# Hybrid decoder step: the samples' reads of the SSD and matrix states with each state as the weights

## The chip, the cores and the metric

The kernel runs on one NeuronCore of one Trainium2 chip, and what is measured is the device time of the whole program in microseconds (us). Before the change it is 1962.44 us, the median of 3 runs (1961.87 to 1963.68).

The engines are named as the profile names them: PE is TensorE's matrix product and PEld its weight load (a second row of the same engine, which runs beside PE), DVE is VectorE, ACT is ScalarE, POOL is GpSimd, and SP is SyncE, which issues the transfers. A matrix product `mm(out, lhsT, rhs)` loads `lhsT` as the weights and streams the columns of `rhs` past them into a PSUM bank.

## The reference, cut to what matters

The program computes one layer of a hybrid decoder: a norm, one wide input projection, two groups of heads side by side (32 SSD heads and 8 mLSTM heads), an output projection, and a gated feed-forward part with a short convolution. It does so for one prompt of 272 tokens (16 learned ones and 256) and for 8 samples of 8 tokens each. The samples carry states of earlier tokens, and this case is about how a sample's tokens read their state:

```python
# SSD, per chunk: Cc are the tokens' read vectors, S the carried state
y = y + jnp.einsum('btgn,bgepn,btge->btgep', Cc, S, jnp.exp(cum))
# mLSTM, per chunk: qc the queries, Cp the carried matrix state, wi the inter-chunk factor
num = jnp.einsum('btsh,bshv->bthv', W, vc) + wi[..., None] * jnp.einsum('bthd,bhdv->bthv', qc, Cp)
```

For a sample b, a head's 8 read vectors (128 long) are multiplied by that sample's own state. The SSD state of two heads is 128 x 128 (128 state entries, 2 x 64 channels), and the matrix state of an mLSTM head is 128 x 256. Every sample has another state, so no two samples share a weight matrix.

## The kernel before

Activations lie transposed: 128 channels on the partitions, 336 tokens as columns. Columns 0 to 255 are the prompt, columns 256 to 319 (`NP` to `ND`) the 64 sample tokens, 8 for each sample, and the rest the learned tokens. All large products are done by `gemm`: a weight block of 8 tiles of 128 x 128 is loaded, ACT and DVE split it into a high and a low part (tiles `hi` and `lo`), and PE runs three products for each tile. These write the banks named `g`. The pool `wp` holds three blocks, and `Feed.next` splits two blocks ahead.

The work of the heads is written as Python generators. `gemm` calls `tick` after every fourth tile, and each tick lets each live generator issue one step, so its small matrix products stand in PE's queue between two groups of `gemm` products. PE and SP keep the order in which the program is written (`manual_schedule`); the instructions of DVE, ACT and POOL are ordered by a scheduler. A small product therefore costs PE its own time, and where it waits, everything behind it on PE waits too.

An mLSTM head (`head`, 8 of them, about 40 to 437 us of the span) makes its read in three places. `spread` on POOL copies the 64 scaled query columns into `qp`, a tile with 32 columns for each sample of which 8 are filled. `read` issues 8 products with `qp[:, b, :]` as weights and the 256 columns of sample b's state as moving columns; four samples fill the four 32-partition strips of one bank `st`, and the second four add to them. ACT copies the bank to `ys`. One step later `turned` transposes the two halves of `ys` on PE, and ACT picks the 64 columns that matter into `yst`. Much later in the head the sums of prompt and samples are made in the two banks `pn` (tag `nm`), and DVE adds `yst` to the sample columns of each.

An SSD unit (`unit`, two heads, 16 of them, about 437 to 800 us) does the same with the state tile `S0` (named S in the profile) and the tile `cp`, which `group` fills once for 8 units: 8 products into a bank `st`, a copy to `ys`, and two steps later one transpose into the bank `pe`, which DVE multiplies into the sample columns of the factor `E`. PE then puts the two products of the prompt's states `S1` and `S2` into the other columns of `pe`, and DVE multiplies those into `E` in a second instruction.

Of the kernel before, what the change touches and what calls it, by code (L numbers as in the profile page):

```python
# [9 lines left out]
F32 = mybir.dt.float32  # L10
F32R = mybir.dt.float32r
AF = mybir.ActivationFunctionType
ALU = mybir.AluOpType
ADD, SUB, MUL, MAX, MIN = ALU.add, ALU.subtract, ALU.mult, ALU.max, ALU.min

P = 128
# [5 lines left out]
NB, TS = 8, 8  # L22
T = TP + NB * TS
NP = 256
NQ = 322
ND = 320
# [23 lines left out]
def hymba_kernel(ctx, tc, cst, xT, w0, w1, wo, wu, wd, shist, s0, c0n, fhist,  # L50
                 yT, conv_o, ssd_o, c_o, m_o, ffn_o):
    nc = tc.nc
    uid = [0]

    def tl(pool, shape, dt=F32, tag=None, **kw):
        uid[0] += 1
        return pool.tile(shape, dt, tag=tag, name=f"{tag}_{uid[0]}", **kw)
# [10 lines left out]
    def mm(out, lhsT, rhs, start=True, stop=True):  # L68
        nc.tensor.matmul(out, lhsT, rhs, start=start, stop=stop)  # L69

    def tt(out, a, b, op):
        nc.vector.tensor_tensor(out, a, b, op=op)  # L72
# [7 lines left out]
    def act(out, a, f, **kw):  # L80
        nc.scalar.activation(out, a, f, **kw)  # L81

    def bank(pool, n, tag="g"):
        return tl(pool, [P, 512], tag=tag)[:, :n]
# [6 lines left out]
    def C(name, i=0, n=None):  # L91
        o, w = _CST[name]
        return cs[:, o + i:o + (w if n is None else i + n)]
# [86 lines left out]
    def start(gen, half=1):  # L180
        gens.append((gen, half))
        next(gen)
# [78 lines left out]
    a = []  # L261
# [26 lines left out]
    with ExitStack() as pa:  # L288
        ca = pa.enter_context(tc.tile_pool(name="ca", reuse_waits="tile", bufs=1))
        pt = pa.enter_context(tc.tile_pool(name="pt", reuse_waits="tile", bufs=1, space=bass.MemoryType.PSUM))  # L290
        pm = pa.enter_context(tc.tile_pool(name="pm", reuse_waits="tile", bufs=2, space=bass.MemoryType.PSUM))
# [17 lines left out]
        sv = lambda t: t[:, NP:ND].rearrange("p (b t) -> p b t", b=NB)  # L309
# [157 lines left out]
            for i in range(2):  # L467
                mm(ps, onesr, x[i], start=i == 0, stop=i == 1)

        def spread(dst, src):  # L470

            nc.gpsimd.tensor_copy(dst[:, 0:4, 0:TS], sv(src)[:, 0:4])
            nc.gpsimd.tensor_copy(dst[:, 4:8, TS:2 * TS], sv(src)[:, 4:8])

        def read(cp, states, n):

            pc = bank(pm, n, "st")
            for b in range(NB):
                o = 32 * (b % 4)
                mm(pc[o:o + 32], cp[:, b, :], states[:, b, :n], start=b < 4, stop=b >= 4)  # L480
            return pc

        def turned(ys, pst=None):

            n = ys.shape[1] // P
            pst = tl(pt, [P, 4, P], tag="tr") if pst is None else pst
            for i in range(n):
                nc.tensor.transpose(pst[:, i, :], ys[:, i * P:(i + 1) * P], C("ident"))
            v = pst[:, :n, :].rearrange("p i (b u t) -> p i u b t", u=4, t=TS)
            return [v[:, i, :2] for i in range(n)]  # L490

        def stacked(d, x, second):

# [9 lines left out]
        def mstack(dst, src, n, second):  # L503

            stacked([dst[32 * i:32 * i + 16, :n] for i in range(3)], src[64:80, 2, :n], second)

        def sb(t):
            return t.rearrange("p (s b t) -> p s b t", s=2, t=TS)

        def masked(dst, src):  # L510
            n = src.shape[2]
# [14 lines left out]

        steps = {-1: 99}

        def heads(ml, qps, h, kf, qf, v0, v1):
            while not gates_done or steps.get(h - 1, 0) < 9:  # L530
                yield
            for n, _ in enumerate(head(ml, qps, h, kf, qf, v0, v1)):
                steps[h] = n
                yield

        def head(ml, qps, h, kf, qf, v0, v1):
            C0 = tl(ml, [P, NB, 257], tag="C0", bufs=2)
            nc.sync.dma_start(C0, c0n[h])
            rowB = tl(ml, [P, 3, T], tag="rowB")
            nc.sync.dma_start(rowB, scr_m[h].unsqueeze(0).to_broadcast([P, 3, T]))  # L540
            qp = qps[h % 2]
            dm = dec[:, 32 + h, :]
            vtok = tl(ml, [P, 3, 258], tag="vtok")
            ksc = tl(ml, [P, 3, P], tag="ksc")
# [10 lines left out]
            act(D[:80, 256:NQ], D[:80, 256:NQ], AF.Exp)  # L555
            qwi = B()
            gt(qwi[:, :ND], qf[:, :ND], rowB[:, 1, :ND], MUL)
            spread(qp, qwi)
            yield

            pq = tl(pt, [P, 4, P], tag="tr").rearrange("p a b -> p (a b)")
# [14 lines left out]
            transpose3(v0, lambda ap, r, c: act(vtok[r, c, 0:128], ap, AF.Copy))  # L576
            yield
            transpose3(v1, lambda ap, r, c: act(vtok[r, c, 128:256], ap, AF.Copy))

            ys = tl(ml, [P, 256], tag="ys")  # L580
            act(ys, read(qp, C0, 256), AF.Copy)
            yield
            yst = tl(ml, [P, 2, 64], tag="yst")
            for i, v in enumerate(turned(ys)):
                act(sb(yst[:, i, :]), v, AF.Copy)

            C1 = tl(ml, [P, 257], tag="C1")
            C2 = tl(ml, [P, 257], tag="C2")
# [23 lines left out]
            for i in range(2):  # L612
                pn = bank(pm, NQ, "nm")
                vs = slice(128 * i, 128 * i + 128)
                for c, (o, n, w) in enumerate(WC):
                    mm(pn[:, o:o + w], vtok[:n, c, vs], W[:n, o:o + w], start=c == 0, stop=False)
                mm(pn[:, 0:128], C1[:, vs], qwi[:, 0:128], start=False, stop=False)
                mm(pn[:, 128:256], C2[:, vs], qwi[:, 128:256], start=False)
                tt(pn[:, NP:ND], pn[:, NP:ND], yst[:, i, :], ADD)
                nums.append(pn)  # L620
                q = B()[:, :NQ]
                act(q, pn, AF.Square)
                sq.append(q)
                yield
# [41 lines left out]
                yml[2 * h + i] = split(yh[i])  # L666

        with tc.tile_pool(name="ml", reuse_waits="tile", bufs=1) as ml:
            qps = [tl(ml, [P, NB, 32], tag=f"qp{i}") for i in range(2)]
            kmt = tl(ml, [80, P], F32R, tag="kmt")  # L670
            vmt = tl(ml, [80, 258], F32R, tag="vmt")
            for t_ in qps + [kmt.bitcast(F32), vmt.bitcast(F32)]:
                nc.gpsimd.memset(t_, 0.0)

            def kqv(h):
                fe = []
                for i, ti in enumerate(KQV(h)):
                    n = NQ if i == 1 else T
                    ps = inproj(ti, n, *((pm, "nm") if h + i == 0 else ()))
                    f = B()[:, :n]  # L680
                    tt(f, ps, R[:, :n], MUL)
                    fe.append(f)
                start(heads(ml, qps, h, *fe), h % 2)

            def oevac(h, i, ps):
                while not ready:
                    yield
                o_ = B()[:, :NQ]
                tt(o_, ps, Rh[:, :NQ], MUL)
                act(o_, o_, AF.Tanh)  # L690
                og[h, i] = o_
                yield

            def ogate(h):
                for i, ti in enumerate(OG(h)):
                    start(oevac(h, i, inproj(ti, NQ)))

            for i in range(2):
                start(oevac(0, i, first[1 + i]))
            for x in stream:  # L700
                (ogate if x[0] == "o" else kqv)(int(x[1]))
            early = {ti: inproj(ti) for ti in (1,)}
            while gens:
                tick()
# [4 lines left out]
        with tc.tile_pool(name="sd", reuse_waits="tile", bufs=1) as sd:  # L709
# [49 lines left out]
            def group(bc, out):  # L759
                for _ in range(3):  # L760
                    yield
                bf, cf = bc
                pq = tl(pt, [P, 4, P], tag="tr").rearrange("p a b -> p (a b)")
                for c, (o, n, w) in enumerate(WC):
                    mm(pq[:n, o:o + w], bf[:, o:o + n], cf[:, o:o + w])
                cb = tl(sd, [P, T], tag="cb")
                tt(cb[:, :256].rearrange("p (c t) -> p c t", c=2),
                   pq[:, :256].rearrange("p (c t) -> p c t", c=2),
                   C("mask").unsqueeze(1).to_broadcast([P, 2, P]), MUL)
                tt(cb[:80, 256:NQ], pq[:80, 256:NQ], C("mask2")[:80, :66], MUL)  # L770
                cp = tl(sd, [P, NB, 32], tag="cp")
                nc.gpsimd.memset(cp, 0.0)
                spread(cp, cf)
                out += [cb, cf, cp]
                yield
                bt = tl(sd, [P, 3, P], tag="bt")
                transpose3(bf, lambda ap, r, c: copy(bt[r, c, :], ap))
                act(bmt[64:80], bt[64:80, 2, :], AF.Copy)
                out.append(bt)

            def unit(j, gc, pad, ps, zz):
# [6 lines left out]
                nc.sync.dma_start(S0, s0[j])  # L788
                yield

                cb, cf, cp = gc[:3]
                Dm = tl(sd, [P, 2, T], tag="Dm")
                hs = slice(2 * j, 2 * j + 2)
                for hh in range(2):
# [6 lines left out]
                tt(Dm[:80, :, 256:NQ], Dm[:80, :, 256:NQ],  # L801
                   cb[:80, None, 256:NQ].to_broadcast([80, 2, 66]), MUL)
                yield
                bt = gc[3]

                xp = tl(sd, [P, 3, P], tag="xp")
                xw = tl(sd, [P, 3, P], tag="xw")
# [21 lines left out]
                act(E[0:64], cmb[0:64, 0, :ND], AF.Exp)  # L829
                act(E[64:128], cmb[64:128, 1, :ND], AF.Exp)  # L830
                yield
                ys = tl(sd, [P, P], tag="ys")
                act(ys, read(cp, S0, P), AF.Copy)
                pi = bank(pm, NQ, "nm")
                for c, (o, n, w) in enumerate(WC):
                    for hh in range(2):
# [21 lines left out]
                   .to_broadcast([P, NB, 2, 64]), MUL)  # L858
                yield
                yield  # L860
                es = sb(E[:, NP:ND])
                pe = bank(pm, 512, "nm")
                tt(es, es, turned(ys, pe[:, 256:384].rearrange("p (a b) -> p a b", a=1))[0], MUL)
                mm(pe[:, 0:128], S1, cf[:, 0:128])
                mm(pe[:, 128:256], S2, cf[:, 128:256])
                tt(E[:, :256], E[:, :256], pe[:, :256], MUL)
                pps = [tl(pm, [P, 512], tag="st").rearrange("p (a b) -> p a b", a=4) for _ in range(2)]
                for i, pp in enumerate(pps):
                    rows = slice(32 * i, 32 * i + 32)
# [274 lines left out]
```

## Time and profile before

| | |
|---|---|
| median of 3 runs | 1962.44 us |
| the profiled execution | 1962.04 us, span 1960.3 us |
| PE busy / PEld busy | 1929.2 us (98%) / 1891.2 us (96%) |
| DVE / ACT / POOL busy | 1240.5 (63%) / 856.3 (44%) / 381.5 us (19%) |
| granted TensorE clock, mean | 0.997 |
| HBM | 162 GB/s over the span |

The span is what the profile sees between the first and the last instruction; 1.7 us of the profiled execution lie around it. A matrix product in plain fp32 is one instruction of the program and shows as two records in the trace, each with its own weight load. The records of PE overlap, since they include the time in the pipe, so the time that a product takes from its successors is read from the distance between starts and not from the length of a record. "x16" at a row's end counts records, and `nm<-cf,S` reads: written bank, then the moving operand, then the weights.

### The profile page before, as it was taken

Reading aid. Unit: us, or ns where it says so; the run is one execution under the profiler, and the core shown is the slowest. Engines: PE = TensorE matmul, PEld = TensorE weight load, DVE = VectorE, ACT = ScalarE, POOL = GpSimd, SP = SyncE. Lnnn points to the kernel's source line nnn. Section 1 sums busy time; section 2 is a strip of 40 time slices with the busy share of each in tenths; the row PEclk is TensorE's granted clock in tenths of the full one; section 3 lists DMA queues with packets and bytes.
Section 4 is the critical chain, followed back from the end, with each engine's and each line's share of the span. In section 5 each row is a group of like instructions: output and inputs, shape, how many; then the busy total and the mean of one; then the engine's idle time right before and its main releaser. Section 6 shows DMA issues by size and latency. Waiting matters only on the chain.

```text
span 1960.3 us, 33606 instructions
## 1 busy us (share of the span) xinstructions
PE 1929.2 (98%) x13302; PEld 1891.2 (96%) x13302; DVE 1240.5 (63%) x2064; ACT 856.3 (44%) x1301; POOL 381.5 (19%) x721
## 2 busy tenths in 40 slices
PE   9999999999999999999999999999999999999997
PEld 8999999999989998999999999999999999999997
DVE  7877676777888788655547666655555556333344
ACT  6355555555444455433334444443334435333332
POOL 1211111212434343211112111111111110111111
PEclk9999999999999999999999999999999999999998
DMA  7545555546554655455554444444444444555553
GB/s 228 178 150 191 175 174 179 193 156 204 185 182 162 199 178 180 150 161 157 163 165 145 154 146 149 153 153 150 148 153 151 152 147 150 148 150 151 152 148 113
DMA packets 94221, 319.68 MB, mean 163 GB/s; under 512 B 10680, under 2 KB 19440, under 8 KB 92016
## 3 DMA queue, kind: packets, MB, share of 16 engines
q1 hardware_dynamic: 93744, 317.26, 50.7%
q8 instruction: 104, 1.70, 0.4%
q10 hardware_dynamic: 320, 0.28, 0.1%
q14 instruction: 53, 0.43, 0.1%
HBM read 294.80 MB, written 22.70 MB: 162 GB/s over the span
## 4 chain that ended last, share of the span: by engine, by line
PE 94%; DVE 3%; DMA 1%; issue 1%; ACT 1%; SPq 0%; DVEq 0%; ACTq 0%
PE g L69 87%; PE st L69 3%; PE nm L69 2%; DMA rowB<-scr_m 1%; PE tr L458 1%; DVE lo L72 1%; DVE blk L78 0%; DVE yb L72 0%; ACT hi L81 0%; DVE blk L72 0%; DMA raw<-in_w 0%; DVE co L78 0%; DVE pad L72 0%; DVE blk L552 0%; PE tr L69 0%
## 5 line engine op out<-in xcount | busy, mean ns | idle before, releaser
L69 PE MATMUL g<-blk,hi 128*128 128x322 f32 (+2 forms) x6240 | 1429.5, 313 | 0.0
L69 PEld LDWEIGHTS g<-blk,hi 128*128 128x128 f32 x6240 | 1054.1, 189 | 5.5 <-issue 4.8
L72 DVE TENSOR_TENSOR lo<-raw,hi 128x1024 fp32r<-128x1024 f32 (+3 forms) x509 | 652.6, 1282 | 464.6 <-ACT hi L81 459.5
L69 PE MATMUL g<-blk,lo 128*128 128x322 f32 (+2 forms) x2992 | 930.8, 311 | 0.0
L81 ACT ACTIVATE hi<-raw 128x1024 fp32r<-128x1024 f32 (+2 forms) x507 | 527.6, 1041 | 760.7 <-PE g L69 521.4
L69 PEld LDWEIGHTS g<-blk,lo 128*128 128x128 f32 x2992 | 563.8, 188 | 0.0
L69 PE MATMUL g<-ah,hi 128*128 128x322 f32 (+1 forms) x832 | 259.6, 312 | 0.0
L69 PE MATMUL g<-ah,lo 128*128 128x322 f32 (+1 forms) x832 | 259.5, 312 | 0.0
L69 PE MATMUL g<-al,hi 128*128 128x322 f32 (+1 forms) x832 | 258.8, 311 | 0.0
L69 PEld LDWEIGHTS g<-ah,hi 128*128 128x128 f32 x832 | 158.2, 190 | 0.1
L69 PEld LDWEIGHTS g<-al,hi 128*128 128x128 f32 x832 | 157.3, 189 | 0.1
L69 PEld LDWEIGHTS g<-ah,lo 128*128 128x128 f32 x832 | 157.1, 189 | 0.0
L72 DVE TENSOR_TENSOR fpad<-g,R 128x256 f32<-128x256 f32 (+2 forms) x264 | 54.6, 263 | 95.2 <-PE g L69 95.1
L235 POOL TENSOR_TENSOR blk<-h 128x322 f32<-128x322 f32 (+1 forms) x28 | 31.0, 1107 | 400.1 <-DVE h L72 231.8
L78 DVE SCALAR_TENSOR_TENSOR fcv<-fpad,fc,fcv 128x336 f32<-128x336 f32 x176 | 99.4, 567 | 3.9 <-ACT fcv L81 0.8
L976 POOL COPY fo<-fpad 128x2 f32<-128x2 f32 x88 | 17.5, 199 | 338.7 <-DVE fpad L72 338.6
L81 ACT ACTIVATE blk<-blk 128x322 fp32r<-128x322 f32 (+6 forms) x118 | 50.4, 450 | 51.7 <-DVE blk L78 20.9
L75 POOL TENSOR_TENSOR blk<-fsg,fcv 128x256 f32<-128x256 f32 x88 | 46.6, 553 | 112.2 <-PE g L69 60.9
L81 ACT ACTIVATE fcv<-fpad,fc 128x336 f32<-128x336 f32 x88 | 57.2, 652 | 0.1
L81 ACT ACTIVATE fsg<-fcv 128x336 f32<-128x336 f32 x44 | 21.3, 484 | 73.1 <-DVE fcv L78 73.1
L236 POOL TENSOR_TENSOR acc<-acc,blk 128x322 f32<-128x322 f32 (+2 forms) x46 | 51.8, 1126 | 2.5
L72 DVE TENSOR_TENSOR blk<-blk,blk 128x322 fp32r<-128x322 f32 (+3 forms) x76 | 38.9, 522 | 18.4 <-ACT blk L81 18.0
(212 smaller groups left out, 1340.0 us busy)
## 6 DMA issues: line engine op xcount, KB each, us to landing
raw<-in_wu SPq DMA_DIRECT2D x176, 512.0 KB, 3.7
raw<-in_w SPq DMA_DIRECT2D x164, 512.0 KB, 4.1
raw<-in_wd SPq DMA_DIRECT2D x80, 512.0 KB, 3.6
raw<-in_wo SPq DMA_DIRECT2D x64, 512.0 KB, 4.1
out_c_o<-co SPq DMA_DIRECT2D x8, 1156.5 KB, 7.4
out_ssd_o<-so SPq DMA_DIRECT2D x16, 576.0 KB, 3.7
C<-in_c0n SPq DMA_DIRECT2D x8, 1028.0 KB, 6.6
S<-in_s SPq DMA_DIRECT2D x16, 512.0 KB, 4.9
```

What stands on the lines that cost most here:

```text
L69: nc.tensor.matmul(out, lhsT, rhs, start=start, stop=stop)
L72: nc.vector.tensor_tensor(out, a, b, op=op)
L75: nc.gpsimd.tensor_tensor(out, a, b, op=op)
L78: nc.vector.scalar_tensor_tensor(out, a, s, b, op0=op0, op1=op1)
L81: nc.scalar.activation(out, a, f, **kw)
L235: eng.tensor_tensor(q, x, x, op=MUL)
L236: eng.tensor_tensor(self.acc[eng], self.acc[eng], q, op=ADD)
L458: nc.tensor.transpose(pst[:n, c, :], src[:, o:o + n], C("ident"))
L976: nc.gpsimd.tensor_copy(fo[:, li, 0:2], pad[:, 256:258])
```

## The change

The tiles `qp`, `cp`, `ys` and `yst` go, with the functions that fill and turn them. A new function `reads` takes each sample's state as the weights (128 x 128) and that sample's 8 tokens as the moving columns, and writes them where the sums stand: 8 products for each half of an mLSTM head, added to the bank `pn`, and 8 products for each SSD unit, into the sample columns of `pe`. In the unit they stand at the step where the old read stood; `pe` is therefore taken at that step, and the product with `E` becomes one DVE instruction over all 320 columns.

```diff
-        def spread(dst, src):
-            nc.gpsimd.tensor_copy(dst[:, 0:4, 0:TS], sv(src)[:, 0:4])
-            nc.gpsimd.tensor_copy(dst[:, 4:8, TS:2 * TS], sv(src)[:, 4:8])
-
-        def read(cp, states, n):
-            pc = bank(pm, n, "st")
+        def reads(ps, states, x, first=True):
             for b in range(NB):
-                o = 32 * (b % 4)
-                mm(pc[o:o + 32], cp[:, b, :], states[:, b, :n], start=b < 4, stop=b >= 4)
-            return pc
-
-        def turned(ys, pst=None):
-            n = ys.shape[1] // P
-            pst = tl(pt, [P, 4, P], tag="tr") if pst is None else pst
-            for i in range(n):
-                nc.tensor.transpose(pst[:, i, :], ys[:, i * P:(i + 1) * P], C("ident"))
-            v = pst[:, :n, :].rearrange("p i (b u t) -> p i u b t", u=4, t=TS)
-            return [v[:, i, :2] for i in range(n)]
+                t = slice(NP + b * TS, NP + b * TS + TS)
+                mm(ps[:, t], states[:, b, :], x[:, t], start=first and b == 0, stop=b == NB - 1)
...
             transpose3(v1, lambda ap, r, c: act(vtok[r, c, 128:256], ap, AF.Copy))
-            ys = tl(ml, [P, 256], tag="ys")
-            act(ys, read(qp, C0, 256), AF.Copy)
-            yield
-            yst = tl(ml, [P, 2, 64], tag="yst")
-            for i, v in enumerate(turned(ys)):
-                act(sb(yst[:, i, :]), v, AF.Copy)
+            yield
...
                 mm(pn[:, 0:128], C1[:, vs], qwi[:, 0:128], start=False, stop=False)
-                mm(pn[:, 128:256], C2[:, vs], qwi[:, 128:256], start=False)
-                tt(pn[:, NP:ND], pn[:, NP:ND], yst[:, i, :], ADD)
+                mm(pn[:, 128:256], C2[:, vs], qwi[:, 128:256], start=False, stop=False)
+                reads(pn, C0[:, :, vs], qwi, False)
...
-                ys = tl(sd, [P, P], tag="ys")
-                act(ys, read(cp, S0, P), AF.Copy)
+                pe = bank(pm, ND, "nm")
+                reads(pe, S0, cf)
                 pi = bank(pm, NQ, "nm")
...
-                es = sb(E[:, NP:ND])
-                pe = bank(pm, 512, "nm")
-                tt(es, es, turned(ys, pe[:, 256:384].rearrange("p (a b) -> p a b", a=1))[0], MUL)
                 mm(pe[:, 0:128], S1, cf[:, 0:128])
                 mm(pe[:, 128:256], S2, cf[:, 128:256])
-                tt(E[:, :256], E[:, :256], pe[:, :256], MUL)
+                tt(E, E, pe, MUL)
```

On PE, in a head's first half of the sums (`nm`), between two groups of `gemm`, these rows stood before:

```order
L69 MATMUL g_1805<-blk_160,lo_1678 128x336
L69 MATMUL st_1836<-vtok_1509,ksc_1510 128x257
L69 MATMUL nm_1839<-blk_1615,vtok_1509 128x128 x2
L69 MATMUL nm_1839<-blk_1615,vtok_1509 128x66
L69 MATMUL nm_1839<-blk_1564,C_341_1774 128x128
L69 MATMUL nm_1839<-blk_1564,C_342_1775 128x128
L69 MATMUL g_1805<-blk_173,hi_1727 128x336
```

At the same place of PE's order the changed kernel has:

```order
L69 MATMUL g_1777<-blk_160,lo_1667 128x336
L69 MATMUL st_1808<-vtok_1500,ksc_1501 128x257
L69 MATMUL nm_1811<-blk_1604,vtok_1500 128x128 x2
L69 MATMUL nm_1811<-blk_1604,vtok_1500 128x66
L69 MATMUL nm_1811<-blk_1555,C_331_1746 128x128
L69 MATMUL nm_1811<-blk_1555,C_332_1747 128x128
L69 MATMUL nm_1811<-blk_1555,C_286_1496 128x8 x8
L69 MATMUL g_1777<-blk_173,hi_1705 128x336
```

One row of 8 products with 8 columns each has come in, behind the prompt's two (C_286 is the samples' state tile, C_331 and C_332 are the prompt's); the second half of the head has the same row. The two places of a head where `read` and `turned` stood have lost their rows.

On PE, in an SSD unit, at the step of the read, these rows stood before (S_980 is the samples' state tile, `Dm` and `xp` belong to the unit's own sums):

```order
L69 MATMUL g_5439<-blk_232,lo_5388 128x322
L69 MATMUL st_5509<-S_980_5335,cp_5283 32x128 x8
L69 MATMUL nm_5519<-Dm_5375,xp_5417 64x128 x4
L69 MATMUL nm_5519<-Dm_5375,xp_5417 64x66 x2
L69 MATMUL st_5526<-xw_5418,bmt_5062 128x128
```

At this place the changed kernel has:

```order
L69 MATMUL g_5391<-blk_232,lo_5340 128x322
L69 MATMUL nm_5460<-cf_5109,S_945_5287 128x8 x8
L69 MATMUL nm_5469<-Dm_5327,xp_5369 64x128 x4
L69 MATMUL nm_5469<-Dm_5327,xp_5369 64x66 x2
L69 MATMUL st_5476<-xw_5370,bmt_5018 128x128
```

The 8 products stay where they were in the order, with weights and moving operand exchanged: 128 weight columns in place of 32, 8 moving columns in place of 128.

On PE, two steps later in the same unit, with the engines that each row waits for, before:

```order
L69 MATMUL g_5555<-blk_232,lo_5479 128x336
L488 MATMUL nm_5628<-cs_71,ys_5508 128x128 [waits Activation_49]
L69 MATMUL nm_5628<-cf_5153,S_1011_5530 128x128 [waits DVE_49,Activation_49]
L69 MATMUL nm_5628<-cf_5153,S_1012_5531 128x128
L69 MATMUL st_5634<-xm_5427,bt_5322 128x512 [waits PE_49,Pool_49]
L69 MATMUL st_5635<-xm_5427,bt_5322 128x512 [waits PE_49]
```

And in the changed kernel:

```order
L69 MATMUL g_5505<-blk_232,lo_5431 128x336
L69 MATMUL nm_5460<-cf_5109,S_975_5480 128x128 [waits Activation_49]
L69 MATMUL nm_5460<-cf_5109,S_976_5481 128x128 [waits DVE_49]
L69 MATMUL st_5581<-xm_5379,bt_5274 128x512 [waits Pool_49]
L69 MATMUL st_5582<-xm_5379,bt_5274 128x512 [waits DVE_49,PE_49]
```

The transpose is gone, and the product with the first prompt state no longer waits for DVE. The product with the second one (S_976, which DVE writes) and the second product into a bank `st` carry waits for DVE now.

## Rows read from the trace of the kernel before

**Rows 1.** The page: busy time, share of the span and instruction count of each engine, and the chain of work that ended last by engine.

```profile
PE 1929.2 (98%) x13302; PEld 1891.2 (96%) x13302; DVE 1240.5 (63%) x2064; ACT 856.3 (44%) x1301; POOL 381.5 (19%) x721
PE 94%; DVE 3%; DMA 1%; issue 1%; ACT 1%; SPq 0%; DVEq 0%; ACTq 0%
```

**Rows 2.** Busy time by stretch, the mLSTM heads and the SSD units: the stretch in us, its length, then busy us (and instructions) of PE, PEld, DVE, ACT and POOL, the granted TensorE clock, DMA share, GB/s.

```profile
40.00:437.00 397.00, 394.60 (x2752) 385.56 (x2751) 290.39 (x514) 206.36 (x372) 69.15 (x109) 1.00 0.53 174
437.00:800.00 363.00, 352.53 (x2609) 327.04 (x2608) 300.22 (x595) 179.55 (x344) 138.58 (x176) 1.00 0.55 181
```

**Rows 3.** Groups of PE instructions by line and shape: weights' rows*columns, moving operand's shape, record count, then busy us, mean ns of one record, idle time before them.

```profile
L69 PE MATMUL st<-S,cp 128*32 128x128 f32 x256 | 10.3, 279 | 0.0
L69 PE MATMUL st<-C,qp 128*32 128x256 f32 x128 | 8.6, 385 | 0.0
L488 PE MATMUL nm<-cs,ys 128*128 128x128 f32 x16 | 4.3, 270 | 0.0
L488 PE MATMUL tr<-cs,ys 128*128 128x128 f32 x16 | 3.1, 272 | 0.0
```

**Rows 4.** PE in order of time in head 1, at the step that transposes the first half of the values: start us, length us, engine, line, operation, operands, shape, records. `g` rows are `gemm`.

```profile
94.12 0.31 PE L69 MATMUL g<-blk,lo 128*128 128x322 f32 x1
94.27 0.49 PE L458 MATMUL tr<-cs,blk 128*128 128x128 f32 x3
94.52 0.55 PE L69 MATMUL g<-blk,hi 128*128 128x322 f32 x2
94.90 0.31 PE L69 MATMUL g<-blk,lo 128*128 128x322 f32 x1
```

**Rows 5.** The same view at the next step of the same head, which transposes the second half of the values and then makes the old read.

```profile
98.00 0.31 PE L69 MATMUL g<-blk,lo 128*128 128x322 f32 x1
...
98.57 1.07 PE L69 MATMUL st<-C,qp 128*32 128x256 f32 x16
99.58 0.56 PE L69 MATMUL g<-blk,hi 128*128 128x322 f32 x2
99.98 0.31 PE L69 MATMUL g<-blk,lo 128*128 128x322 f32 x1
```

**Rows 6.** PEld, the weight loads, in order of time in the first half of the sums of head 1: the last two loads of the products with the values `vtok`, then four with the prompt's states, then `gemm`.

```profile
108.35 0.30 PEld L69 LDWEIGHTS nm<-blk,vtok 80*128 80x128 f32 x2
...
108.57 0.53 PEld L69 LDWEIGHTS nm<-blk,C 128*128 128x128 f32 x4
109.02 0.30 PEld L69 LDWEIGHTS g<-blk,hi 128*128 128x128 f32 x2
```

**Rows 7.** PE beside it: the two records of the product with 66 moving columns, and the first of the next product.

```profile
108.46 0.34 PE L69 MATMUL nm<-blk,vtok 80*128 80x66 f32 x2
108.63 0.33 PE L69 MATMUL nm<-blk,C 128*128 128x128 f32 x1
```

**Rows 8.** PE in order of time at the read of the first SSD unit.

```profile
477.70 0.30 PE L69 MATMUL g<-blk,lo 128*128 128x322 f32 x1
477.94 0.64 PE L69 MATMUL st<-S,cp 128*32 128x128 f32 x16
478.51 0.78 PE L69 MATMUL nm<-Dm,xp 128*64 128x128 f32 x12
```

**Rows 9.** PE in order of time two steps later in the same unit, at the transpose of the read; in brackets idle time before, and what ended it.

```profile
487.19 0.32 PE L69 MATMUL g<-blk,lo 128*128 128x336 f32 x1
487.35 0.27 PE L488 MATMUL nm<-cs,ys 128*128 128x128 f32 x1
488.31 0.68 PE L69 MATMUL nm<-cf,S 128*128 128x128 f32 x4 [0.69 <-DVE pad L72]
488.93 1.13 PE L69 MATMUL st<-xm,bt 32*128 32x512 f32 x4
```

**Rows 10.** What PE waited for in the whole span: us in total, times, longest us.

```profile
PE nm L69 <- DVE pad L72: 9.0, 14, 0.7
PE tr L458 <- DVE blk L72: 2.0, 3, 1.1
...
PE nm L69 <- DVE E L72: 1.5, 2, 1.1
```

**Rows 11.** Groups of weight loads by shape: rows*columns of the weights, record count, busy us, mean ns of one record. L488 is a transpose, where the data are the weights.

```profile
L69 PEld LDWEIGHTS nm<-cf,S 128*128 128x128 f32 x64 | 8.3, 190 | 14.5 <-issue 13.1 <-ACT hi L81 1.3
...
L488 PEld LDWEIGHTS nm<-cs,ys 128*128 128x128 f32 x16 | 2.3, 141 | 0.0
```

**Rows 12.** Busy time by stretch, columns as in rows 2: a wait of PE among the heads, and two stretches at the program's end. The granted clock is the third number from the right.

```profile
178.00:181.00 3.00, 1.92 (x14) 1.67 (x13) 3.00 (x8) 1.50 (x5) 1.07 (x2) 1.00 0.22 79
1945.00:1950.00 5.00, 1.34 (x6) 0.61 (x5) 4.73 (x8) 0.79 (x2) 2.27 (x2) 1.00 0.13 49
1950.00:1953.00 3.00, 0.00 (x0) 0.00 (x0) 2.97 (x4) 0.00 (x0) 1.51 (x2) 0.55 0.84 314
```

**Rows 13.** PE in order of time at the program's start: the 12 products that only warm the engine.

```profile
1.17 3.69 PE L69 MATMUL g<-R 128*128 128x336 f32 x12 [1.17 <-POOL R L98]
```

**Rows 14.** The chain that ended last, in order of time: the `gemm` products behind the block of rows 9 (start us, us, what).

```profile
490.53 7.09 PE g L69 x48
```

**Rows 15.** DVE in order of time beside rows 9, and, earlier, at the writing of the second prompt state `S2` (named S).

```profile
482.10 0.46 DVE L78 SCALAR_TENSOR_TENSOR S<-S,dec,st 128x64 f32<-128x64 f32 x2
...
487.96 0.21 DVE L72 TENSOR_TENSOR E<-E,nm 128x64 f32<-128x64 f32 x1
```

## The prediction before the run

> **What bounds the kernel now.** Read the page's first lines first: PE is busy for 98% of the span, and the chain of work that ended last runs over PE for 94% [rows 1]. The view by stretches says the same of the two stages that the change touches: PE is busy for 394.6 of 397 us among the heads and for 352.5 of 363 among the SSD units, while DVE, ACT and POOL have room [rows 2]. So a microsecond that is put into PE's queue or taken out of it appears in the time, and work taken from ACT and POOL (the copies to ys and yst, spread) and the additions on DVE are worth nothing by themselves. Of PE's 10.5 idle us in the SSD stage, nearly all are one wait in each unit [rows 10], at one place [rows 9]. For all else the question is only how long PE works on the old read and on the new one. For that I read the distance between gemm products on both sides of a block, in the view in order of time. A gemm product takes 0.148 us of PE: 48 of them fill 7.09 us [rows 14].
>
> **Heads: what goes.** Two steps of head 1 differ only in the old read. The step without it spans 0.78 us, from the gemm product at 94.12 to the one at 94.90 [rows 4]; the step with it spans 1.98 us, from 98.00 to 99.98 [rows 5]. The read takes 1.20 us, 9.6 in 8 heads. It is cheap because four samples stand in four strips: 16 records of 256 columns need about one us. The three transposes of rows 4 take 0.78 - 3 x 0.148 = 0.34 us, 0.11 each. The 16 transposes of ys [rows 3], two in a head, take 2 x 0.11 x 8 = 1.8 us. Together 11.4 us go.
>
> **Heads: what comes.** A product in fp32 has two records: the old read's 8 products in each of 8 heads are 128 records [rows 3]. The new 16 products of a head are therefore 32 weight loads of 128 columns and 32 runs of 8 columns, and 256 of each in all heads. No row of before has 8 moving columns, so I bound the pair. Beside a product with 66 columns the two weight loads start 0.22 us apart from what follows, 0.11 each (108.35 to 108.57), and the four loads of products with 128 columns take 0.45 us, again 0.11 each (108.57 to 109.02) [rows 6, 7]. Halving the columns did not shorten the pair: the load sets the pace there, and 8 columns hide behind it just as 66 do. I take 0.111 us, the mean of these six (0.67 / 6 = 0.112, rounded down for the two digits of the rows). The lower bound is the weight load of a transpose, whose record is 141 ns against 190 ns for an ordinary one [rows 11]: 0.049 us less, 0.06 for a pair. The upper bound is a whole load's record with nothing beside it, 0.19 us. I choose 0.111 because rows 6 show the same shape, type and neighbour (the new reads stand right behind these four loads), and the upper one would need loads that never overlap, which rows 6 exclude for their case. 256 x 0.111 = 28.4 us. Heads: +28.4 - 11.4 = +17.0 us.
>
> The Trainium skill says otherwise of such pairs: its page "TensorE: Matmul & The Clock Gate", section "Back-to-back issue gap", gives about 81 ns for a sustained stream of weight load and product with 128 columns. The rows here have 111 ns for it; the sum would be about +3.6 us by 81 ns, and the measurement decides.
>
> **SSD units: the read.** Before, from the last gemm product to the unit's own products: 477.70 to 478.51, 0.81 us [rows 8]. Of the 0.24 us in front of the first strip, 0.148 belong to gemm and 0.09 to the change to strips, which the unit's products (two strips) still pay. After: 0.15 for gemm, 15 steps of 0.111 = 1.67 from the first read to the last, 0.01 for its 8 columns, 0.09 for strips: 1.92 us, 1.11 more. 16 units: +17.7 us.
>
> **SSD units: the transpose and its wait.** Before, from 487.19 to the products with xm at 488.93: 1.74 us, of which 0.69 are PE's wait [rows 9]. The row names DVE's pad, but what PE needs is the product with E that reads the transposed block out of pe: it runs on DVE from 487.96 for 0.21 us [rows 15], and PE goes on 0.1 us behind it. After the change nothing of this step reads pe before PE has written it. Left are 0.16 for gemm's product, 4 x 0.111 for the two products, 0.09 for the strips of xm: 0.69 us. So 0.36 us go beside the wait, 5.7 in 16 units, and the waits themselves, 9.0 + 1.5 us [rows 10]: 16.2 in all. What is late next? The second prompt state is written by DVE at 482.10 [rows 15], 5 us early, and the new wait of a product with xm is for an st bank whose readers on DVE belong to the same early group. DVE's order also changes: the products with E and the two sums now stand ahead of a split into lo; 48 gemm products, 7.09 us [rows 14], lie between this place and the first use of that split in PE's order. I price both at nothing; if that cover were gone, the wait would come back (below). SSD: +17.7 - 16.2 = +1.5 us.
>
> **The sum.** +17.0 + 1.5 = +18.5 us on the profiled execution's 1962.04 us (span 1960.3 and 1.7 around it) gives 1980.5. The median of the runs is 0.4 above that execution, so 1981 us, 0.9% slower. The ends: 0.108 us a pair gives +17.0, and the 2.0 us that PE waits at the heads' transposes [rows 10] may vanish or double, since DVE's order and the arrival of transfers shift: 1977. With the 8 columns never hidden (0.111 + 0.007 = 0.118) it is +22.0, with 2 us of waits 1986.5.
>
> **Rivals.**
> *Loads get quick when almost no columns stream beside them (faster than before).* At 0.06 us a pair, as the transposes' loads suggest [rows 11], the heads have +15.6 - 11.4 = +4.2; a unit's read is 0.25 + 15 x 0.061 - 0.81 = +0.36, 5.7 in 16, against 16.2: -10.5. Sum -6.3, 1956 us. It decides from the point where a pair falls under 0.074 us: the sum is 496 pairs (256 and 16 x 15) less 36.6 us (11.4, 16.2 and 16 x 0.56), and is zero there. For it: transposes do it. Against it: rows 6 show no shortening at 66 columns, and the new weights are ordinary ones. 6%. Halfway, at 0.086 us, the sum is +6.1, 1968.5 us, and up to 0.082 us it would be within the bound of no change. 6%, of which 4 lie there. By the 81 ns of the Trainium skill's "TensorE: Matmul & The Clock Gate" ("Back-to-back issue gap") this case would end at 1966 us.
> *The wait is replaced.* If PE must wait as long for DVE at the second state, the st bank or the later split as it did for E, the 10.5 us are not won: 1991.5 us. For it: two new waits in the order, and DVE is busy for 300 of the 363 us [rows 2]. Against it: the times above. 5%.
> *The clock falls.* In a stretch of 16 pairs PE streams almost nothing for 1.8 us. At the program's start the lower of the two levels, 1.2 GHz, shows: 12 products with 336 columns in 3.69 us, 0.31 each, about twice what gemm pays [rows 13]. If after each of the 32 blocks 12 gemm products ran at that level, 32 x 12 x 0.15 = 58 us are added: 2039. Against it: among the heads PE stood idle for 1.1 us of 178 to 181 us at a granted clock of 1.00, and at the end it is still 1.00 over 1945 to 1950, with PE busy for 1.34 of 5 us, before it falls to 0.55 [rows 10, 12]. 4%.
> *Loads and columns do not overlap at all*, 0.19 us a pair: heads +48.6 - 11.4, units 16 x 2.29 - 16.2, sum +57.6, 2020 us. 3%.
>
> **How the numbers follow.** The forecast keeps 76%; its own range is 1977 to 1986.5. The range that should hold the time 8 times in 10 takes in the wait that comes back and some error in the entry to each block: 1974 to 1992. No change means within 0.2%, 3.9 us, about what a measurement of this kernel can tell. Faster by more: 6%, the quick loads. Within: 4%, the part of the halfway case. Slower: 90%.
>
> **What the profile after would show.** Right: in PEld's rows the loads of nm<-blk,C with 128 columns and 8 moving ones follow each other at 0.11 us, and a unit's read block (gemm to Dm) lasts 1.9 us where it was 0.8; PE's wait at the products with cf is gone from the waits; the stretch of the heads is 17 us longer, that of the units 1 or 2. Wrong: loads at 0.06 or 0.08 us; a new wait of PE for DVE at cf or xm, which would put the units' stretch at +10 or more; a granted clock under 1.00 among the heads; or gemm products that start later than their predecessors ask, which would mean that a block of weights came late.

## The result and the profile after

The changed kernel takes 1983.12 us, the median of 4 runs (1982.64 to 1984.08), against 1962.54 us for the kernel before on the same chip (4 runs, 1961.87 to 1963.68). The ratio is 1.0105 with a 95% interval of 1.0087 to 1.0122: slower by 20.6 us, or 17 to 24 by the interval. The profiled execution took 1982.78 us with a span of 1980.7. Its page, busy time by engine and the chain that ended last, answers to [rows 1]:

```profile
PE 1960.7 (99%) x13398; PEld 1938.6 (98%) x13398; DVE 1225.7 (62%) x2032; ACT 851.1 (43%) x1261; POOL 398.0 (20%) x697
PE 94%; DVE 3%; DMA 2%; ACT 1%; issue 1%; SPq 0%; DVEq 0%; ACTq 0%
```

DVE and ACT have less to do than before (14.8 and 5.2 us less), and the program is longer all the same: PE is the engine that counts, and its weight loads are busy for 47 us more. The weight loads of PE in the first half of the sums of head 1 answer to [rows 6]; the 20 loads are the prompt's four and the 16 new ones:

```profile
106.75 2.31 PEld L69 LDWEIGHTS nm<-blk,C 128*128 128x128 f32 x20
108.98 0.30 PEld L69 LDWEIGHTS g<-blk,hi 128*128 128x128 f32 x2
```

From the first of the 20 to the load of gemm lie 2.23 us, 0.1115 for each. This is the price that the four loads of [rows 6] had (0.1125), although 16 of the 20 now have only 8 columns behind them. PE at the read of the first SSD unit answers to [rows 8]:

```profile
494.69 0.31 PE L69 MATMUL g<-blk,lo 128*128 128x322 f32 x1
494.83 1.85 PE L69 MATMUL nm<-cf,S 128*128 128x8 f32 x16
496.61 0.78 PE L69 MATMUL nm<-Dm,xp 128*64 128x128 f32 x12
```

1.92 us lie between the gemm product and the unit's own products, where it was 0.81. Two steps later the transpose of [rows 9] and the wait behind it are gone:

```profile
505.32 0.31 PE L69 MATMUL g<-blk,lo 128*128 128x336 f32 x1
505.47 0.60 PE L69 MATMUL nm<-cf,S 128*128 128x128 f32 x4
506.00 1.13 PE L69 MATMUL st<-xm,bt 32*128 32x512 f32 x4
```

That is 0.68 us up to the products with xm, where it was 1.74. What PE waits for now, in the whole span (us, times, longest), answers to [rows 10]:

```profile
PE tr L458 <- DVE blk L72: 1.8, 2, 1.0
PE nm L69 <- DVE lo L72: 1.6, 2, 1.0
...
PE st L69 <- DVE vmt L72: 0.4, 1, 0.4
...
PE st L69 <- ACT vs L81: 0.3, 1, 0.3
```

The two lines for the SSD units (9.0 and 1.5 us) have no successor. The two lines for `st` are new and small: they stand at the product with vmt of two heads. The stretch that holds both sums of head 1, and one with a unit's read (columns as in [rows 12], the granted clock third from the right), show that the clock did not move:

```profile
100.00:115.00 15.00, 15.00 (x114) 14.89 (x112) 7.40 (x12) 6.51 (x12) 0.14 (x2) 1.00 0.33 108
495.00:500.00 5.00, 5.00 (x47) 4.91 (x47) 2.56 (x10) 3.56 (x10) 1.93 (x1) 1.00 0.61 206
```

How far the kernel has fallen behind is read from the chain that ended last. Three of its runs of gemm products stand at the same places of both kernels: ahead of the heads' reads, behind the heads, and behind the last unit (start us, us, what). In the kernel before:

```profile
39.74 32.76 PE g L69 x216
...
436.75 21.99 PE g L69 x144
...
798.91 1145.82 PE g L69 x7734
```

In the changed kernel, where the last run is broken once:

```profile
39.41 32.69 PE g L69 x216
...
453.71 21.94 PE g L69 x144
...
817.75 207.07 PE g L69 x1391
...
1026.76 4.09 DMA fpad<-in_xT
...
1030.94 0.51 DVE h L72
...
1032.74 932.71 PE g L69 x6294
```

The changed kernel starts 0.33 us early, is 16.96 us late behind the heads and 18.84 us late behind the last unit: the heads took 17.3 us more and the units 1.9. The break is the turn from the output projection to the up projection. There PE had to wait for the last residual tile of x, whose transfer was issued 0.7 us later against the gemm products than before (1026.76 us here, 1007.18 there, less the 18.84); against the same gemm products in the trace of before it costs 0.8 us. The rest of the 20.4 us between the two spans, 0.8, is spread thinly over the gemm products behind it, and is no more than what the runs of one kernel differ by.

### The profile page after: what moved, and what is told of

It reads as the page before. It is cut to its first block, busy times and chain, and to the rows that moved or that the text cites. A ratio compares the mean times of both kernels' runs of the same rounds, so it can differ in the third digit from the quotient of the medians.

```text
span 1980.7 us, 33680 instructions
## 1 busy us (share of the span) xinstructions
PE 1960.7 (99%) x13398; PEld 1938.6 (98%) x13398; DVE 1225.7 (62%) x2032; ACT 851.1 (43%) x1261; POOL 398.0 (20%) x697
## 4 chain that ended last, share of the span: by engine, by line
PE 94%; DVE 3%; DMA 2%; ACT 1%; issue 1%; SPq 0%; DVEq 0%; ACTq 0%
PE g L69 85%; PE nm L69 5%; PE st L69 2%; DMA rowB<-scr_m 1%; PE tr L458 1%; DVE lo L72 1%; DVE blk L78 1%; DMA raw<-in_w 0%; DVE co L78 0%; DVE blk L72 0%; DVE yb L72 0%; ACT blk L81 0%; DVE blk L532 0%; DMA fpad<-in_xT 0%; ACT hi L81 0%
## 5 line engine op out<-in xcount | busy, mean ns | idle before, releaser
L72 DVE TENSOR_TENSOR lo<-raw,hi 128x1024 fp32r<-128x1024 f32 (+3 forms) x509 | 632.3, 1242 | 440.1 <-ACT hi L81 436.3
L942 POOL COPY fo<-fpad 128x2 f32<-128x2 f32 x88 | 17.4, 197 | 333.1 <-DVE fpad L72 333.1
L236 POOL TENSOR_TENSOR acc<-acc,blk 128x322 f32<-128x322 f32 (+2 forms) x46 | 70.1, 1524 | 3.5
```

Source lines behind the costliest of these rows:

```text
L236: eng.tensor_tensor(self.acc[eng], self.acc[eng], q, op=ADD)
L942: nc.gpsimd.tensor_copy(fo[:, li, 0:2], pad[:, 256:258])
```

## Experiments

**The heads alone.** The new reads in `head`, the old ones in `unit`:

```diff
 # head as in the changed kernel
...
+                reads(pn, C0[:, :, vs], qwi, False)
...
 # unit as before
                 ys = tl(sd, [P, P], tag="ys")
                 act(ys, read(cp, S0, P), AF.Copy)
```

> The new reads in the mLSTM heads alone, the SSD units as before. Theory (a read costs PE one weight load of 128 columns, 0.112 us a record): the heads' stretch is longer by 256 x 0.112 - 11.4 = 17.3 us, PE's wait at the products with cf stays at about 10 us, and the time is 1980 us. Rival (the loss comes from the units, from the order of DVE or the banks there): under 1970 us.

Measured in one run: 1982.82 us. The loads of the first half of the sums keep the pace of the changed kernel (2.24 us for 20), PE's wait in the units is as it was before, and the chain has the three places again:

```profile
108.01 2.31 PEld L69 LDWEIGHTS nm<-blk,C 128*128 128x128 f32 x20
110.25 0.30 PEld L69 LDWEIGHTS g<-blk,hi 128*128 128x128 f32 x2
```

```profile
PE nm L69 <- DVE pad L72: 9.3, 14, 1.0
```

```profile
40.67 32.69 PE g L69 x216
...
455.08 21.94 PE g L69 x144
...
819.21 205.87 PE g L69 x1386
```

This run is 0.93 us late ahead of the heads' reads and 18.33 behind the heads: they took 17.4 us, where 17.3 were expected. The total is 3 us over what was expected, and not because of the reads: 0.9 us were lost before them, and 2.0 in the units, whose blocks of PE are those of the kernel before. One run's total can thus be a few us off, and what a place costs is read between the lines of the chain.

**The units alone.** The same the other way round:

```diff
 # head as before; in unit
...
-                act(ys, read(cp, S0, P), AF.Copy)
+                pe = bank(pm, ND, "nm")
+                reads(pe, S0, cf)
...
-                tt(E[:, :256], E[:, :256], pe[:, :256], MUL)
+                tt(E, E, pe, MUL)
```

> The new reads in the SSD units alone, the heads as before. Theory: the read block of a unit grows by 1.11 us, the block two steps later shrinks by 1.0 us since PE no longer waits there for DVE; in 16 units +1.5 us, so about 1964 us. Rival (the two changes are not independent, or the wait is replaced by another): 1974 us or more.

Measured in one run: 1968.01 us, 4 more than expected and 6 under the rival's bound. The first unit's read, and the chain behind the heads and behind the last unit:

```profile
478.78 0.31 PE L69 MATMUL g<-blk,lo 128*128 128x322 f32 x1
478.93 1.85 PE L69 MATMUL nm<-cf,S 128*128 128x8 f32 x16
480.70 0.55 PE L69 MATMUL nm<-Dm,xp 128*64 128x128 f32 x6
```

```profile
437.82 21.99 PE g L69 x144
...
801.70 206.50 PE g L69 x1388
```

The read spans 1.92 us as in the changed kernel. This execution was already 1.07 us late behind the heads (437.82 against 436.75), ahead of which nothing differs from the kernel before. From there to 801.70 it loses 801.70 - 798.91 - 1.07 = 1.7 us, near the 1.5 expected. Another 3.3 us came behind the last unit, where no read stands: 1.7 of them at the turn to the up projection, the rest spread over the gemm products behind it. The wait at the turn can't be put down to this execution alone. By the starts of the same gemm products in the traces, it costs 0.5 to 1.9 us in all seven kernels that have the new reads in some place, and under 0.1 us in the three executions without them. Why it comes with the reads is open.

**64 columns for 8.** Each read moves all 64 sample columns past its state; every sample's sums then hold all 8 reads, so this kernel computes something else and serves only for its time:

```diff
-                t = slice(NP + b * TS, NP + b * TS + TS)
-                mm(ps[:, t], states[:, b, :], x[:, t], start=first and b == 0, stop=b == NB - 1)
+                mm(ps[:, NP:ND], states[:, b, :], x[:, NP:ND], start=first and b == 0, stop=b == NB - 1)
```

> Every read of the changed kernel moves all 64 sample columns past its state in place of its own 8, so that every sample's sums hold the reads of all 8 states, which is another computation. Theory (the weight load sets the pace, columns up to about 0.1 us hide behind it): records still start 0.112 us apart and the time stays within 3 us of the changed kernel's 1983. Rival (a load and its columns follow each other): 56 more columns of 0.83 ns, 0.047 us for each of 512 records, 24 us more, 2007 us.

Measured in one run: 1986.24 us. PE at the first unit's read:

```profile
496.67 0.31 PE L69 MATMUL g<-blk,lo 128*128 128x322 f32 x1
496.81 1.90 PE L69 MATMUL nm<-cf,S 128*128 128x64 f32 x16
498.64 0.78 PE L69 MATMUL nm<-Dm,xp 128*64 128x128 f32 x12
```

1.97 us in place of 1.92: of eight times as many columns 0.05 us show, 0.03 behind the first record and 0.02 behind the last; in between, the records start 0.112 us apart in both kernels. The rival asked for 16 x 0.047 = 0.75 us more here. The load sets the pace, and up to 64 columns are free but for the two ends of a block. The time is 3.1 us over the changed kernel's, just beyond the 3 expected; 16 x 0.05 = 0.8 us of it are these ends, and 1.8 us were lost ahead of the heads' reads (the chain's run of 216 gemm products starts at 41.20 against 39.41 us).

**The order of two things in the kernel before.** Only this exchange, in `unit`; the products with S1 and S2 now stand ahead of the transpose:

```diff
                 pe = bank(pm, 512, "nm")
-                tt(es, es, turned(ys, pe[:, 256:384].rearrange("p (a b) -> p a b", a=1))[0], MUL)
                 mm(pe[:, 0:128], S1, cf[:, 0:128])
                 mm(pe[:, 128:256], S2, cf[:, 128:256])
+                tt(es, es, turned(ys, pe[:, 256:384].rearrange("p (a b) -> p a b", a=1))[0], MUL)
```

> The kernel before, with one exchange in the SSD units: the two products with the prompt's states go into pe ahead of the transpose of ys, and nothing else is changed. Theory (the only thing that the change wins in the units beside PE's work is PE's wait for DVE behind the transpose, 10.5 us in all): that wait is gone, 1952 us, faster than both kernels. Rival (another wait takes its place, at the products with xm or at the next transposes): within 3 us of 1962.

Measured: 1949.29 us, the median of 4 runs, ratio to the kernel before 0.9918 (0.9896 to 0.9941). A second set of runs, on another chip:

> The kernel before with the transpose of ys behind the two products, once more, on the same chip as the one with four strips in the units. Theory: the block is 2.16 us in place of 3.03, 13.9 us less, 1949 us. Rival (the first run of it was favoured by its chip): nearer to 1952 us, by the 10.5 us of recorded waits alone.

Measured: 1948.09 us, ratio 0.9924 (0.9910 to 0.9939). PE at the place of [rows 9] in this second run:

```profile
487.70 0.31 PE L69 MATMUL g<-blk,lo 128*128 128x336 f32 x1
487.85 0.60 PE L69 MATMUL nm<-cf,S 128*128 128x128 f32 x4
488.30 0.27 PE L488 MATMUL nm<-cs,ys 128*128 128x128 f32 x1
488.50 1.13 PE L69 MATMUL st<-xm,bt 32*128 32x512 f32 x4
```

And its chain behind the heads and behind the last unit:

```profile
437.26 21.99 PE g L69 x144
...
785.09 1144.60 PE g L69 x7734
```

From gemm to xm 0.80 us with the transpose still there, against 1.74 in the first unit before and 0.68 without a transpose. No line for this place is left in PE's waits. The wait of before came from two writers of `pe` with a reader between them: PE had to let DVE read the transposed columns before it wrote the others. With both writes ahead of the read nobody waits. Whether the bank or the program's tile makes PE wait there, no run separates. The first expectation of the gain was too small: it counted the idle time that the waits list, 10.5 us. The block up to the next gemm product shrank from 3.03 us in most units (3.10 in the first) to 2.16, and the 16 blocks together by 14.3 us; the chain has the same, 347.83 us between its two places against 362.16 before. The recorded idle time begins only at the end of the transpose's record, 0.27 us long, while a transpose holds up its successor by 0.11; the stall is longer than its line.

**Two strips, four strips.** The changed kernel, with each state's 128 weight columns cut into two products of 64, or four of 32, into the strips of the same bank:

```diff
-                mm(ps[:, t], states[:, b, :], x[:, t], start=first and b == 0, stop=b == NB - 1)
+                for o in range(0, P, 32):   # 64 for two strips
+                    mm(ps[o:o + 32, t], states[:, b, o:o + 32], x[:, t], start=first and b == 0, stop=b == NB - 1)
```

> Each read of the changed kernel is cut into two products, the state's first 64 columns as weights into partitions 0 to 63 of the bank and the other 64 into partitions 64 to 127; the computation is the same. Theory (a load costs its columns, and loads into different strips of the array run side by side): a pair of loads takes 0.056 us in place of 0.111, 28 us less for 512, and every block pays about 0.09 us at its start and in the heads at its end for the change of shape, 4 us more: 1959 us. Rival (each load has a fixed price, or the strips load one after the other): 1983 us or more.

> The same with four products of 32 weight columns each, into the four 32-partition strips. Theory: four loads side by side take 0.028 us by their columns and about as much by their issue (strips of the old read started 0.007 us apart): 0.03 to 0.055 us a group in place of 0.111, 29 to 41 us less, 4 us more for the changes of shape: 1946 to 1958 us, faster than the kernel before. Rival (no side by side, or a price for each of the 2048 records): 1983 us or more; at 0.112 us a record it would be near 2155.

Measured: two strips 1965.32 us in one run; four strips 1951.64 us, the median of 4 runs, ratio to the kernel before 0.9941 (0.9924 to 0.9958). PE at the first unit's read with two strips:

```profile
489.59 0.30 PE L69 MATMUL g<-blk,lo 128*128 128x322 f32 x1
489.83 1.11 PE L69 MATMUL nm<-cf,S 128*64 128x8 f32 x32
490.78 0.76 PE L69 MATMUL nm<-Dm,xp 128*64 128x128 f32 x12
```

And with four:

```profile
481.11 0.30 PE L69 MATMUL g<-blk,lo 128*128 128x322 f32 x1
481.35 0.72 PE L69 MATMUL nm<-cf,S 128*32 128x8 f32 x64
482.00 0.78 PE L69 MATMUL nm<-Dm,xp 128*64 128x128 f32 x12
```

The read spans 1.19 and 0.89 us, where whole states took 1.92 and the old read 0.81. From the first record to the unit's own products, two strips take 0.95 us, 0.95 / 16 = 0.059 for a pair of loads that have 128 columns together. With four strips it is 0.65; less 0.09, the prediction's price for the change of shape, 0.56, and a group of four loads takes 0.56 / 16 = 0.035 us (0.041 if nothing is taken off). Four times as many records, and a third of the time: a price for each record is excluded, loads into different column strips run side by side, and each costs about its own columns. In a head the 20 loads of 2.23 us become 68:

```profile
107.18 1.28 PEld L69 LDWEIGHTS nm<-blk,C 128*128 128x128 f32 x68
108.48 0.30 PEld L69 LDWEIGHTS g<-blk,hi 128*128 128x128 f32 x2
```

1.30 us to gemm's load; less 0.45 for the prompt's four, 0.85 for 16 groups, 0.053 each. The difference to the unit's 0.035 is put down to the change of shape into the strips and out of them, 0.85 - 0.56 = 0.3 us a block, where the expectations had about 0.18. The expectation for four strips held. Two strips came out at 1965 and not at 1959 us, and the change of shape is only a part of that: from gemm product to gemm product, a head's block shrank by 0.58 us against the changed kernel and a unit's by 0.76, about 21 us for 16 blocks of each kind where 24 were expected, and the time fell by 17.8. The other 3 us or so lie outside these blocks, ahead of the heads and among them; a single run doesn't tell whether they would come again.

**Four strips in the units, the old read in the heads.** In a head the old read cost 1.42 us and four strips cost 2 x 0.85, so the old one was kept there:

```diff
 # head as before; unit as in the changed kernel, with reads in four strips
...
+                for o in range(0, P, 32):
+                    mm(ps[o:o + 32, t], states[:, b, o:o + 32], x[:, t], start=first and b == 0, stop=b == NB - 1)
```

> The heads read as before, the SSD units as in the kernel with four strips. Theory (the places add up, each by its own block): a unit's read block is 2.28 us against 2.21 before, the block two steps later 2.05 against 3.03, 0.90 us less in each of 16 units, 14.4 us, and the heads keep their cheaper read: 1948 to 1950 us, at or a little under the kernel that only turns the order round. Rival (the gain of four strips belongs to the heads, or DVE takes the place of the wait): 1955 us or more.

Measured: 1949.61 us, the median of 4 runs, ratio to the kernel before 0.9932 (0.9916 to 0.9949). Its chain behind the heads and behind the last unit:

```profile
435.81 21.99 PE g L69 x144
...
783.15 206.29 PE g L69 x1387
```

Behind the last unit four strips are 1.9 us ahead of the kernel with the exchanged order on the same chip (785.09), but 1.45 of them were there behind the heads (435.81 against 437.26), whose code is the same in both. In the units four strips gain 0.5 us on the exchanged order and 14.8 on the kernel before, where 14.4 were expected. In the whole time the two can't be told apart (1949.61 and 1948.09 us, with overlapping intervals). Both beat the kernel before and the changed one; the exchange of two lines does it without any new read.

## Why the prediction was right, and where it was off

The forecast was 1981 us, +18.5 us worked out against the profiled execution; measured are 1983.12 us, and +20.4 between the two spans.

**PE bounds.** Right. DVE and ACT lost 14.8 and 5.2 us of work in the changed kernel and no time followed it, and the exchanged order gained 14 us with the same work on them. What PE's queue gained or lost came out in the time.

**Heads, +17.0.** Right. The pair of load and product was taken as 0.111 us; it measured 0.1115 in the sums of head 1, and 64 columns in place of 8 left it so. The choice between the bounds 0.06 and 0.19 carried the forecast, and it was sound for the reason given: beside a product with 66 columns the loads had kept 0.11 us. By the chain the heads took 16.96 + 0.33 = 17.3 us more, and 17.4 with the heads changed alone.

**Units, +1.5.** Right. A read block of 1.92 us was forecast and measured, the later block was forecast at 0.69 us and measured at 0.68. Behind the last unit the kernel is 18.84 us late, 16.96 of it from before the units, so they added 1.9; changed alone they added 1.7.

**What it left out.** Two small terms are not in its sum. At the vmt product of two heads PE waits for 0.64 us in all. The same two waits stand in all five kernels with the new reads in the heads and in none with the old ones, so they come with the edit there; the likely cause, argued and not tried, is that the way to this product is 1.4 us shorter without the read and the two transposes, and that ACT and DVE need that time for vs and vmt. Other small waits went, so that the heads' total is hardly touched. And at the turn to the up projection PE waits 0.8 us for a transfer that it had not waited for before, as it does in every kernel with the new reads. Neither was found by the questions that the prediction asked of DVE at the products with cf and xm, where indeed nothing waits. The measured 20.4 us and the 18.5 of the sum thus differ by 0.3 in the heads, 0.4 in the units and 1.6 behind them, less the 0.3 by which this execution started early.

**The rivals.** Quick loads are excluded, and so are the halfway price of 0.086 us and the 0.19 of loads and columns that never overlap: the pair took 0.1115 us. The Trainium skill's figure for a stream of pairs ("TensorE: Matmul & The Clock Gate", "Back-to-back issue gap", about 81 ns) did not hold for these fp32 pairs, where the rows show 111. What holds is the section "LDWEIGHTS (loading the stationary operand)" of the same page of the Trainium skill, by which a load's time goes with the columns of its weights; by its formula the estimate for 128 columns is 107 ns. The rows have 111, and 59 for 64 columns in two strips. The wait did not come back: the waits list has no line for cf or xm. The clock kept its upper level, 2.4 GHz: a granted clock of 1.00 in the stretches of the reads. The price that the prediction gave to the lower level goes by the pace of the first products alone [rows 13]; the view's granted clock over 0 to 5 us reads 1.00.

## What to carry to other kernels

Exchanging weights and moving operand to save columns pays nothing once the weight load sets the pace: count the loads and their columns, then the moving columns. Where few columns are moved, cut the weights into the four column strips; the loads then run side by side (0.035 us for 128 columns in place of 0.111). Count the change of shape too, about 0.3 us a block in the heads here: there the old read with its transposes, at 1.42 us a head, stayed cheaper than four strips at 1.7. And where PE waits for a reader of a bank between two of its own writes, put both writes ahead of the read before changing anything else.

## What the runs showed of the hardware that was not expected

- Loads of 32 weight columns into the four column strips overlap each other, with 8 moving columns behind each: 64 records in 0.65 us, against 16 records with full weights in 1.78.
- The idle time in the waits list understates a stall behind a short product: 0.66 us a unit were listed, and 0.9 went when the wait went.
- POOL's sums of squares (acc) take 1.52 us a piece in the changed kernel and 1.13 before. The kernel with the exchanged order has 1.52 as well, although POOL's work is unchanged there, and the kernel with the new reads in the heads alone has 1.12. It is on no path; its cause wasn't tried.
